# Normalizing rows before the transposes, with ScalarE forming the scaled high parts, in a hybrid S5/FNet encoder block on one Trainium2 core

## The chip, the cores and the metric

The kernel runs on one core of a Trainium2 chip. The metric is the device time of one execution in microseconds (us), the median of several runs. Engines are named as in the profile: PE is TensorE (PEld its weight loads), DVE is VectorE, ACT is ScalarE, POOL is GpSimd, SP is the queue that issues most loads. Rows that end in q (SPq, ACTq) are a queue's own instructions.

## The reference, cut to what matters

The model width is 2048, the sequence 512, the batch 1. All arrays are float32.

```python
mod = silu(c) @ w_ada + b_ada                       # six sections of 2048: sh_m, sc_m, g_m, sh_f, sc_f, g_f
h = rms_norm(x, norm_mix) * (1.0 + sc_m) + sh_m     # rms_norm: x * rsqrt(mean(x*x, -1) + 1e-6) * g
proj = h @ w_in                                     # widths: 512 (S5), 1536 (FNet), 2048 + 2048 (two gates)
merged = sigmoid(gate_s5) * (y_s5 @ w_branch_s5) + sigmoid(gate_fn) * (y_fn @ w_branch_fnet)
x = x + g_m * (merged @ w_out)                      # y_s5: bidirectional state-space scan; y_fn: 2-D DFT
h2 = rms_norm(x, norm_ffn) * (1.0 + sc_f) + sh_f
a, b = split(h2 @ w_ffn_in); x = x + g_f * ((silu(a) * b) @ w_ffn_out)
return rms_norm(x, norm_final)
```

## The kernel before, in words

Every large product is made of three fp32r matmuls (`mm3`, lines 207 to 209): each operand is split into a high part (`hi`, rounded to fp32r by ACT, line 124) and a low part (`lo`, source minus high part, by DVE, line 125). Activations are held transposed, as 16 pairs of tiles `h_hl[k]` of 128 channels x 512 positions (`actA` for k below 4, else `actB`).

Work is a list of steps. A step has a job (a load into a ring of buffers, then a preparation such as a split) and a function that issues the matmuls. `run_plan` walks the list and issues loads as soon as a ring slot is free: `raw` has 5 slots, `araw` 8, split weights (`whi`, `wlo`) 3. PE and POOL keep the order in which the program is written; the order on ACT, DVE and SP is set by the scheduler of the build.

The start, up to about 115 us, is this. `x_job(t)` loads a tile of 128 rows of x in two halves, transposes it on PE into `mg` (named `xT` in the rows), and squares it on ACT to get row sums. `x_rstd` turns all 512 sums into reciprocal roots and spreads them by matmuls into `rb` (128 x 512, the same in every partition). The scale section `sc_m` of `mod` is computed in five blocks of 256 to 512 columns, of which the first is done by PE (`ada_pe`) and the others by DVE, ACT and POOL (`ada_job`: DVE multiplies and adds, line 295; ACT scales and POOL adds a share of it, lines 289 and 291), and is summed over partitions by PE (line 340). Each finished block lets `form_hs(k)` make `h_hl[k]` from x times scale, still without the shift. Six column blocks of `w_in` (`start_w`) are multiplied as the k become ready. DVE does the scaled x (`scaled_x`, line 424, into `htmp`).

Then come column blocks 6 to 11 of the first gate (`ntile`). Beside them the shift section is computed (same `ada_job`), DVE works through small operations for the S5 tables (line 527), and during block 11 `form_h(k)` makes `h_hl[k]` anew, with the shift. After it `u_fn` computes the S5 input from eight weight tiles, here called u0 to u7. Between its matmuls PE transposes nine small tiles `dup` (line 670, written by ACT, lines 661 and 662, three buffers). SP loads the S5 arrays `R` (line 721) into memory that `mg` and the `dup` tiles used before. From `R`, DVE and POOL build the tables of eight S5 batches (lines 738 to 787), which PE takes up at lines 827, 863 and 901 to 904.

Much later, at 927 to 1127 us, block n of the product with `w_out` (lines 1342 to 1357) adds the old x, which comes back from DRAM (`sxT`) in tiles `xr`. Beside it DVE still computes scale and shift sections through the five `raw` slots.

Of the kernel before, what the change touches and what calls it, by code (L numbers as in the profile page):

```python
# [11 lines left out]
F32 = mybir.dt.float32  # L12
# [39 lines left out]
def encoder_block(ctx: ExitStack, tc: tile.TileContext, x, c, w_ada, b_ada, norm_mix, w_in,  # L52
# [174 lines left out]
    pv = ps_m((P, P))  # L227
    PE.transpose(pv, rows, ident)
    V.tensor_copy(vec, pv)
# [75 lines left out]
    def ada_pe(width, then):  # L305
# [5 lines left out]
        def job(q):  # L311
# [5 lines left out]
            def fn(r):  # L317
# [7 lines left out]
                if q == parts - 1:  # L325
                    n = width // P
                    V.tensor_reduce(out=mod[1][:, 0:n], in_=pt[0], op=ALU.add, axis=mybir.AxisListType.X)
                    V.tensor_tensor(out=mod[1][:, 0:n], in0=mod[1][:, 0:n], in1=vec[:, KT:KT + n], op=ALU.add)
                    then()
# [43 lines left out]
    rb = y_pool.tile([P, S], F32, name="rb")  # L373

    def x_job(t):
# [9 lines left out]
        def prep(r):  # L385
# [10 lines left out]
            for h in range(2):  # L396
                junk = ring.tile([P, D // 2], F32R, tag="whi", bufs=WH_BUFS, name="junk")
                A.activation(out=junk, in_=r[h], func=AF.Square, accum_out=xs_[:, h, t:t + 1])
            return None

        return Job(load, prep, raw=(("raw" if t < 2 else "araw", 2),), keep=())

    def x_rstd(_):
        v, r, t = (xs_[:, i, :] for i in (2, 3, 1))
        V.tensor_tensor(out=v, in0=xs_[:, 0, :], in1=xs_[:, 1, :], op=ALU.add)
        V.tensor_scalar(out=v, in0=v, scalar1=1.0 / D, scalar2=EPS, op0=ALU.mult, op1=ALU.add)
        newton_rsqrt(r, v, t)
        bcast_cols(r, rb)
# [6 lines left out]
    def form_hs(k):  # L415
# [3 lines left out]
        split(hi, lo, scaled_x(k))  # L419
        h_hl[k] = (hi, lo)  # L420

    def scaled_x(k):
        tmp = cpool.tile([P, S], F32, tag="tmp", bufs=3, name="htmp")
        V.scalar_tensor_tensor(out=tmp, in0=mg[:, k, :], scalar=s_mix[:, k:k + 1], in1=rb,
                               op0=ALU.mult, op1=ALU.mult)
        return tmp

    def form_h(k):
        add_split(h_hl[k], scaled_x(k), mod[0][:, k:k + 1])
# [30 lines left out]
    for i, (k0, nk) in enumerate(blocks):  # L460
# [4 lines left out]
        blk = ada_pe(nk * P, then) if i == 0 else ada_steps(1, k0 * P, nk * P, True, then)  # L465
# [4 lines left out]
        if i == 0:  # L470
            start_steps += [(x_job(t), nop) for t in range(4)]
            start_steps += blk[:-1] + [(None, x_rstd)] + blk[-1:] + ws
# [843 lines left out]
    def wo_open(_):  # L1316
# [8 lines left out]
        x1["x"] = {}  # L1325

    step(None, wo_open)

    def xT_load(n):
        xr = x1["p"].tile([P, S], F32, tag="xr", bufs=3, name="xr")  # L1330
        A.dma_start(out=xr, in_=sxT[n])
        x1["x"][n] = xr
# [444 lines left out]
```

## Time and profile before

| | |
|---|---|
| median of 3 runs (lowest, highest) | 2557.15 us (2549.0, 2558.74) |
| profiled execution: time, span | 2563.62 us, 2561.7 us |
| PE busy, share of the span | 2437.8 us, 95% |
| DVE busy | 1674.1 us, 65% |
| ACT busy | 1030.5 us, 40% |
| POOL busy | 605.9 us, 24% |
| PE, DVE busy at 30 to 130 us | 82.90, 90.96 us |
| PE, DVE busy at 130 to 200 us | 60.72, 65.53 us |

The span is that of one execution, 1.9 us shorter than its own time, and that time is 6.5 us above the median. PE is busy almost throughout, but a busy PE can run at the lower of its two clocks (1.2 instead of 2.4 GHz), which the windows show as a granted clock below 1.00. The first 200 us are where PE has gaps and DVE has almost none.

### The profile page before, as it was taken

Reading aid. Unit: us, or ns where it says so; the run is one execution under the profiler, and the core shown is the slowest. Engines: PE = TensorE matmul, PEld = TensorE weight load, DVE = VectorE, ACT = ScalarE, POOL = GpSimd, SP = SyncE. Lnnn points to the kernel's source line nnn. Section 1 sums busy time; section 2 is a strip of 40 time slices with the busy share of each in tenths; the row PEclk is TensorE's granted clock in tenths of the full one; section 3 lists DMA queues with packets and bytes.
Section 4 is the critical chain, followed back from the end, with each engine's and each line's share of the span. In section 5 each row is a group of like instructions: output and inputs, shape, how many; then the busy total and the mean of one; then the engine's idle time right before and its main releaser. Section 6 shows DMA issues by size and latency. Waiting matters only on the chain.

```text
span 2561.7 us, 37880 instructions
## 1 busy us (share of the span) xinstructions
PE 2437.8 (95%) x14475; PEld 2157.9 (84%) x14475; DVE 1674.1 (65%) x2454; ACT 1030.5 (40%) x1465; POOL 605.9 (24%) x683
## 2 busy tenths in 40 slices
PE   6989799899999899999999999999999999999997
PEld 5767687788888787778999999999999988888886
DVE  6998466537766987778567676776766643344335
ACT  4434333343223422244455555554555532223223
POOL 2441989600004510000222222222222230001001
PEclk8989999999999999999999999999999999999998
DMA  9796522558764678863888888888888984444442
GB/s 325 256 310 146 128 77 84 173 151 264 259 216 148 178 222 268 276 222 115 198 204 208 210 212 209 215 209 214 214 201 193 208 290 144 148 136 153 144 147 90
DMA packets 440901, 497.37 MB, mean 194 GB/s; under 512 B 51056, under 2 KB 336256, under 8 KB 440720
## 3 DMA queue, kind: packets, MB, share of 16 engines
q1 hardware_dynamic: 359472, 384.68, 47.6%
q0 software_dynamic: 52960, 79.78, 16.9%
q10 hardware_dynamic: 28288, 30.49, 4.1%
q8 instruction: 113, 1.85, 0.3%
q14 instruction: 68, 0.56, 0.1%
HBM read 395.17 MB, written 40.90 MB: 170 GB/s over the span
## 4 chain that ended last, share of the span: by engine, by line
PE 50%; DVE 18%; DMA 14%; issue 7%; POOL 6%; ACT 4%; SPq 0%; ACTq 0%; DVEq 0%; POOLq 0%
DMA raw<-in_w_ada_dram 6%; PE ps_acc L207 4%; PE ps_acc L208 4%; PE ps_acc L209 4%; DMA raw<-in_w_out_dram 3%; PE ps_acc L1656 3%; PE ps_acc L1655 3%; PE ps_acc L1657 3%; DVE ada L295 3%; DVE wlo L125 3%; PE ps_acc L1509 3%; PE ps_acc L1510 3%; PE ps_acc L1511 3%; DMA raw<-in_w_in_dram 2%; DVE lT L125 2%
## 5 line engine op out<-in xcount | busy, mean ns | idle before, releaser
L125 DVE TENSOR_TENSOR wlo<-raw,whi 128x1024 fp32r<-128x1024 f32 (+2 forms) x264 | 324.8, 1232 | 191.1 <-ACT whi L124 190.3
L1463 POOL DMA_DIRECT2D wlo<-raw x160 | 192.4, 1203 | 948.6 <-ACT wlo L1462 566.6
L124 ACT CAST whi<-raw 128x1024 fp32r<-128x1024 f32 (+2 forms) x264 | 260.5, 988 | 326.9 <-DMA raw<-in_w_out_dram 104.6
L209 PE MATMUL ps_acc<-actB,wlo 128*128 128x512 f32 x816 | 324.9, 398 | 8.1 <-DVE wlo L125 8.1
L207 PE MATMUL ps_acc<-actB,whi 128*128 128x512 f32 x816 | 329.9, 404 | 1.9 <-ACT whi L124 1.5
L208 PE MATMUL ps_acc<-actB,whi 128*128 128x512 f32 x816 | 324.1, 397 | 0.3 <-DVE actB L125 0.3
L124 ACT CAST hT<-raw 128x1024 fp32r<-128x1024 f32 x160 | 167.6, 1047 | 258.4 <-DVE raw L1474 174.0
L295 DVE SCALAR_TENSOR_TENSOR ada<-raw,c_s,ada 128x512 f32<-128x512 f32 x240 | 181.2, 755 | 134.2 <-DMA raw<-in_w_ada_dram 130.7
L125 DVE TENSOR_TENSOR lT<-raw,hT 128x1024 fp32r<-128x1024 f32 x160 | 195.5, 1222 | 79.2 <-ACT hT L124 78.9
L125 DVE TENSOR_TENSOR actA<-ab,actA 128x512 fp32r<-128x512 f32 x88 | 61.8, 704 | 263.2 <-ACT actA L124 263.2
L209 PEld LDWEIGHTS ps_acc<-actB,wlo 128*128 128x128 f32 x816 | 156.9, 192 | 45.3 <-DVE wlo L125 11.3
L207 PEld LDWEIGHTS ps_acc<-actB,whi 128*128 128x128 f32 x816 | 157.8, 193 | 37.0 <-ACT whi L124 2.7
L208 PEld LDWEIGHTS ps_acc<-actB,whi 128*128 128x128 f32 x816 | 157.1, 193 | 31.4 <-DVE actB L125 0.6
L124 ACT CAST actA<-ab 128x512 fp32r<-128x512 f32 x88 | 54.8, 623 | 315.3 <-PE ps_m L1656 305.6
L1461 ACT CAST whi<-raw 128x768 fp32r<-128x768 f32 x160 | 133.0, 831 | 90.7 <-PE ps_acc L1510 71.8
L1656 PE MATMUL ps_acc<-wlo,actA 128*128 128x512 f32 x352 | 137.2, 390 | 0.8 <-DVE wlo L125 0.8
L1655 PE MATMUL ps_acc<-whi,actA 128*128 128x512 f32 x352 | 137.2, 390 | 0.2 <-DVE ab L1521 0.2
L1657 PE MATMUL ps_acc<-whi,actA 128*128 128x512 f32 x352 | 137.0, 389 | 0.0
L1462 ACT ACTIVATE wlo<-raw 128x768 fp32r<-128x768 f32 x160 | 134.4, 840 | 0.0
L1675 POOL TENSOR_TENSOR actB<-actB 128x512 f32<-128x512 f32 x15 | 23.3, 1573 | 428.0 <-ACT fot L1673 428.0
L1472 DVE TENSOR_TENSOR raw<-raw 128x512 f32<-128x512 f32 x160 | 110.6, 691 | 18.9 <-DMA wlo<-raw 14.0
L207 PE MATMUL ps_acc<-actA,whi 128*128 128x512 f32 x272 | 112.9, 415 | 2.1 <-ACT actA L124 2.1
(475 smaller groups left out, 7049.2 us busy)
## 6 DMA issues: line engine op xcount, KB each, us to landing
raw<-in_w_ffn_in_dram SPq DMA_DIRECT2D x168, 512.0 KB
raw<-in_w_ada_dram SPq DMA_DIRECT2D x128, 512.0 KB
wlo<-raw POOLq DMA_DIRECT2D x160, 384.0 KB, 5.7
raw<-in_w_in_dram SPq DMA_DIRECT2D x108, 512.0 KB
raw<-in_w_ffn_out_dram SPq DMA_DIRECT2D x88, 512.0 KB
araw<-in_w_ada_dram SPq DMA_DIRECT2D x64, 512.0 KB
ab<-sg SPq DMA_DIRECT2D x88, 256.0 KB
raw<-in_w_out_dram SPq DMA_DIRECT2D x32, 512.0 KB
```

The lines of the kernel that those rows point to most:

```text
L124: A.copy(hi, src)
L125: V.tensor_tensor(out=lo, in0=src, in1=hi.bitcast(F32), op=ALU.subtract)
L207: PE.matmul(o, whi, ahi, start=start, stop=False)
L208: PE.matmul(o, whi, alo, start=False, stop=False)
L209: PE.matmul(o, wlo, ahi, start=False, stop=stop)
L295: V.scalar_tensor_tensor(out=acc, in0=r[:, k, :], scalar=sc, in1=acc, op0=ALU.mult, op1=ALU.add)
L1461: A.copy(hi, r[:, :, 0:3])
L1462: A.activation(out=lo, in_=r[:, :, 0:3], func=AF.Copy, scale=-1.0)
L1463: G.dma_start(out=lo, in_=r[:, :, 0:3], accum_op=ALU.add)
L1655: PE.matmul(o, gh[:, ts_], hi[:, cs], start=(k == 0), stop=False)
L1656: PE.matmul(o, gh[:, ts_], lo[:, cs], start=False, stop=False)
L1657: PE.matmul(o, gl[:, ts_], hi[:, cs], start=False, stop=(k == NF - 1))
```

## The change

Four things change. The first scale block (four `araw` loads) is loaded before x, and its matmuls come first on PE. Each tile of x is normalized as it lies: the reciprocal root is formed for each tile by itself, DVE multiplies the first half of the rows and ACT the second, and the transposes follow, so `mg` holds normalized x, and `rb` is gone. In `form_hs` ACT writes the high part directly from `mg` with the scale, and DVE the low part, with no `htmp`; in `form_h` ACT writes `htmp` (scale and shift), and again the high part. At the product with `w_out` the stored x must be multiplied back by its root mean square: `sd` is spread by matmuls at its beginning, and POOL multiplies each `xr` tile by it. A scheduler barrier stands behind the x tiles.

```diff
-    pv = ps_m((P, P))
-    PE.transpose(pv, rows, ident)
-    V.tensor_copy(vec, pv)
+    def vec_t():
+        pv = ps_m((P, P))
+        PE.transpose(pv, rows, ident)
+        V.tensor_copy(vec, pv)
...
                 if q == parts - 1:
+                    vec_t()
...
-        def prep(r):
+        def fn(r):
+            s0, s1, v, rstd = (xs_[:, i, t:t + 1] for i in range(4))
+            for h in range(2):
+                junk = ring.tile([P, D // 2], F32R, tag="whi", bufs=WH_BUFS, name="junk")
+                A.activation(out=junk, in_=r[h], func=AF.Square, accum_out=xs_[:, h, t:t + 1])
+            V.tensor_tensor(out=v, in0=s0, in1=s1, op=ALU.add)
+            V.tensor_scalar(out=v, in0=v, scalar1=1.0 / D, scalar2=EPS, op0=ALU.mult, op1=ALU.add)
+            newton_rsqrt(rstd, v, s1)
+            V.tensor_scalar(out=r[0], in0=r[0], scalar1=rstd, scalar2=None, op0=ALU.mult)
+            A.activation(out=r[1], in_=r[1], func=AF.Copy, scale=rstd)
             for q in range(4):
...
+            V.tensor_tensor(out=s0, in0=v, in1=rstd, op=ALU.mult)
+        return Job(load, lambda r: r, raw=(("raw" if t < 2 else "araw", 2),), keep=(), hold=True), fn
...
-        split(hi, lo, scaled_x(k))
+        sc = s_mix[:, k:k + 1]
+        A.activation(out=hi, in_=mg[:, k, :], func=AF.Copy, scale=sc)
+        V.scalar_tensor_tensor(out=lo, in0=mg[:, k, :], scalar=sc, in1=hi.bitcast(F32),
+                               op0=ALU.mult, op1=ALU.subtract)
...
-    def scaled_x(k):
+    def form_h(k):
         tmp = cpool.tile([P, S], F32, tag="tmp", bufs=3, name="htmp")
-        V.scalar_tensor_tensor(out=tmp, in0=mg[:, k, :], scalar=s_mix[:, k:k + 1], in1=rb,
-                               op0=ALU.mult, op1=ALU.mult)
-        return tmp
-    def form_h(k):
-        add_split(h_hl[k], scaled_x(k), mod[0][:, k:k + 1])
+        A.activation(out=tmp, in_=mg[:, k, :], func=AF.Identity, scale=s_mix[:, k:k + 1],
+                     bias=mod[0][:, k:k + 1])
+        split(*h_hl[k], tmp)
...
-            start_steps += [(x_job(t), nop) for t in range(4)]
-            start_steps += blk[:-1] + [(None, x_rstd)] + blk[-1:] + ws
+            start_steps += blk + [x_job(t) for t in range(4)]
+            barriers.add(len(start_steps))
+            start_steps += [(None, lambda _, then=then: (tc.no_sync_barrier(), then()))] + ws
...
+        x1["sd"] = p.tile([P, S], F32, name="sd")
+        bcast_cols(xs_[:, 0, :], x1["sd"])
...
         A.dma_start(out=xr, in_=sxT[n])
+        G.tensor_tensor(out=xr, in0=xr, in1=x1["sd"], op=ALU.mult)
```

On ACT at the start of the program, before the change, the squares and copies of the x tiles (`junk`, `xT`) stand in this order up to the first weight split and the first high part of h (`actA`):

```order
L398 ACTIVATE junk,xs<-raw 128x1024 x4
L398 ACTIVATE junk,xs<-xr 128x1024
L393 COPY xT<-ps_acc 128x4x128
L398 ACTIVATE junk,xs<-xr 128x1024 x2
L393 COPY xT<-ps_acc 128x4x128
L398 ACTIVATE junk,xs<-xr 128x1024
L393 COPY xT<-ps_acc 128x4x128 x2
L235 ACT_TABLE_LOAD
L235 ACTIVATE xs<-xs 128x4
```

With the change, the second half of the same stretch on ACT, from the last squares to the first high part, reads (L397 multiplies half a tile of x, L237 is a square root):

```order
L397 ACTIVATE raw<-raw,xs 128x1024
L392 ACTIVATE junk,xs<-xr 128x1024 x2
L405 COPY xT<-ps_acc 128x4x128
L397 ACTIVATE xr<-xr,xs 128x1024
L237 ACTIVATE xs<-xs 128x1
L405 COPY xT<-ps_acc 128x4x128
L397 ACTIVATE xr<-xr,xs 128x1024
L405 COPY xT<-ps_acc 128x4x128
L124 CAST whi<-raw 128x768
L423 ACTIVATE actA<-xT,s_mix 128x512
```

Four multiplications and four square roots now stand between the squares, and the copies wait for transposes that wait for a multiplication.

On ACT during block 11, before the change, the high parts of `form_h` (L128), the weight splits and the `dup` tiles are mixed:

```order
L128 ACTIVATE actB<-htmp,mod_91 128x512 x3
L124 CAST whi<-raw 128x1024
L128 ACTIVATE actB<-htmp,mod_91 128x512 x3
L661 ACTIVATE dup<-q_1124 64x64
L128 ACTIVATE actB<-htmp,mod_91 128x512
L662 ACTIVATE dup<-q_1124 64x64
L124 CAST whi<-raw 128x1024
L661 ACTIVATE dup<-q_1123 64x64
```

With the change the same place on ACT has `htmp` and high parts of all 16 k in a row, with one weight split between them; these are its last rows and what follows:

```order
L430 ACTIVATE htmp<-xT,mod_88,s_mix 128x512 x2
L124 CAST actB<-htmp 128x512 x2
L455 COPY sg<-ps_acc 128x512
L124 CAST whi<-raw 128x1024
L458 DMA sg_100<-sg 128x512
L665 ACTIVATE dup<-q_1122 64x64
L666 ACTIVATE dup<-q_1122 64x64
L124 CAST whi<-raw 128x1024
L665 ACTIVATE dup<-q_1121 64x64
```

The fourth `dup` tile moved from behind the tenth high part to behind the sixteenth, the copy of block 11 and a weight split. On SP, before the change, the loads of `R` stand so between the loads of u0 to u7 (128x2x512) and of the blocks after them:

```order
L137 DMA raw<-in_w_in_dram 128x2x512 x7
L721 DMA R<-in_s_b_re_dram 64x32x16
L137 DMA raw<-in_w_in_dram 128x2x512
L721 DMA R<-in_s_b_im_dram 64x32x16
L137 DMA raw<-in_w_in_dram 128x8x128 x2
L721 DMA R<-in_s_b_im_dram 64x32x16
```

and with the change so:

```order
L137 DMA raw<-in_w_in_dram 128x2x512 x8
L137 DMA raw<-in_w_in_dram 128x8x128
L725 DMA R<-in_s_b_re_dram 64x32x16
L725 DMA R<-in_s_b_im_dram 64x32x16 x2
L137 DMA raw<-in_w_in_dram 128x8x128
L725 DMA R<-in_s_b_re_dram 64x32x16 x2
```

The first `R` load moved behind two more weight loads. Behind the second load of 128x8x128 stood six `R` loads before, and five stand there now. Behind these places the order on all engines is the same as before, but for the spreading matmuls and the POOL multiplications at the product with `w_out`.

## Rows read from the trace of the kernel before

**Rows 1.** The page, part 1: busy time, share of the span, instructions.

```profile
PE 2437.8 (95%) x14475; PEld 2157.9 (84%) x14475; DVE 1674.1 (65%) x2454; ACT 1030.5 (40%) x1465; POOL 605.9 (24%) x683
```

**Rows 2.** Windows: stretch, length, busy time of each engine (instructions), PEclk, DMA share, GB/s.

```profile
10.00:20.00 10.00, 10.00 (x81) 9.79 (x79) 7.78 (x14) 8.08 (x15) 0.00 (x0) 1.00 1.06 376
...
30.00:130.00 100.00, 82.90 (x333) 66.97 (x334) 90.96 (x118) 44.65 (x70) 42.38 (x31) 0.87 0.81 273
130.00:200.00 70.00, 60.72 (x249) 47.71 (x248) 65.53 (x172) 24.81 (x39) 29.80 (x19) 0.90 0.91 305
```

**Rows 3.** Groups by shape on DVE at 28 to 135 us: busy, mean ns | idle.

```profile
L424 DVE SCALAR_TENSOR_TENSOR htmp<-xT,s_mix,rb 128x512 f32<-128x512 f32 x16 | 13.0, 840 | 0.0
```

**Rows 4.** The chain that ended last, within the first 330 us: start, us, what.

```profile
126.41 6.93 DMA ls<-in_s_log_step_dram
```

**Rows 5.** Timeline of the first 62 us: start, us, engine, line, operation [idle before].

```profile
5.42 1.04 ACT L398 ACTIVATE junk<-raw 128x1024 fp32r<-128x1024 f32 x1
...
14.13 3.84 PE L390 MATMUL ps_acc<-ident,xr 128*128 128x128 f32 x32
...
20.22 0.20 ACT L235 ACTIVATE xs<-xs 128x4 f32<-128x4 f32 x1
...
21.27 0.16 DVE L240 TENSOR_TENSOR xs<-xs 128x4 f32<-128x4 f32 x1
...
21.36 0.96 DVE L125 TENSOR_TENSOR wlo<-raw,whi 128x768 fp32r<-128x768 f32 x1
...
23.37 2.05 PE L246 MATMUL ps_m<-ident,xs 128*128 128x128 f32 x8
...
30.74 0.79 PE L207 MATMUL ps_acc<-actA,whi 128*128 128x512 f32 x1 [2.11 <-ACT actA L124]
```

**Rows 6.** Groups by shape on ACT at 5 to 31 us: count | busy, mean ns | idle.

```profile
L235 ACT ACT_TABLE_LOAD x1 | 1.3, 1283 | 0.3 <-DVE xs L406 0.3
```

**Rows 7.** Timeline of ACT, DVE and PE at 196 to 262 us.

```profile
201.12 0.58 ACT L452 COPY sg<-ps_acc 128x512 f32<-128x512 f32 x1
...
216.84 1.39 ACT L128 ACTIVATE actB<-htmp,mod 128x512 fp32r<-128x512 f32 x2 [2.16 <-DVE htmp L424]
...
206.30 0.75 DVE L424 SCALAR_TENSOR_TENSOR htmp<-xT,s_mix,rb 128x512 f32<-128x512 f32 x1 [1.85 <-DMA sg<-sg]
...
219.44 0.27 PE L670 MATMUL ps_m<-ident,dup 64*128 64x64 f32 x1
```

**Rows 8.** The chain at 200 to 640 us, around the S5 tables.

```profile
233.28 0.68 SPq L721
...
242.07 4.85 DMA R<-in_s_b_re_dram
...
316.60 0.69 PE ps_accb L902 x2
```

**Rows 9.** Waits of PE at 230 to 620 us: waited for, us in total, times, longest.

```profile
PE ps_accb L902 <- POOL S L887: 11.9, 2, 11.4
```

**Rows 10.** Windows of PE alone: stretch, length, busy (instructions), PEclk, DMA share, GB/s.

```profile
320.00:330.00 10.00, 10.00 (x39) 0.67 0.00 0
330.00:340.00 10.00, 10.00 (x56) 1.00 0.25 79
```

**Rows 11.** The chain at 1006 to 1032 us, in the product with w_out.

```profile
1014.84 1.06 ACT whi L124
1015.92 1.24 DVE wlo L125
1017.18 3.90 DMA raw<-in_w_out_dram
...
1030.24 0.67 DVE x1T L1345
```

**Rows 12.** Instructions on the araw tiles to 130 us: ns min/median/max, first and last start.

```profile
L295 DVE SCALAR_TENSOR_TENSOR ada<-araw,c_s,ada x42: 478/752/1789, 31.0 to 125.5; 128x512 f32<-128x512 f32 x35, 128x256 f32<-128x256 f32 x7
L291 POOL TENSOR_TENSOR ada<-ada,araw x27: 777/1614/2153, 32.0 to 123.2; 128x512 f32<-128x512 f32 x20, 128x256 f32<-128x256 f32 x7
```

More of the change, by code (lines that the diff above doesn't have):

```diff
@@ L372, in encoder_block @@
     xs_ = cpool.tile([P, 4, 4], F32, name="xs")
-    rb = y_pool.tile([P, S], F32, name="rb")
     def x_job(t):
@@ L395, in prep @@
                     V.tensor_copy(dst, pt)
[L396 to L408, printed above, removed]
+            V.tensor_tensor(out=s0, in0=v, in1=rstd, op=ALU.mult)
+        return Job(load, lambda r: r, raw=(("raw" if t < 2 else "araw", 2),), keep=(), hold=True), fn
     h_hl = [None] * KT
@@ L463, in then @@
                 form_hs(k)
-        blk = ada_pe(nk * P, then) if i == 0 else ada_steps(1, k0 * P, nk * P, True, then)
+        blk = ada_pe(nk * P, lambda: None) if i == 0 else ada_steps(1, k0 * P, nk * P, True, then)
         ws = []
```

## The prediction

> **What bounds the kernel now.** The page comes first: PE is busy for 95% of the span [rows 1], so a change pays only where PE waits or what PE waits for comes sooner. The windows show where that is: at 30 to 130 us PE is busy for 82.90 of 100 us at a granted clock of 0.87, and DVE for 90.96; at 130 to 200 us the two have 60.72 and 65.53 of 70 [rows 2]. In these 170 us DVE is the fullest engine. It is not the only limit: the chain leaves it for DMA and POOL in places, such as the 6.93 us for a small S5 array at 126 us [rows 4].
>
> Next comes a stretch in which PE does not set the end, though it looks busy. The chain at 200 to 640 us runs from the load of R, which lands about 247 us (242.07 + 4.85), through POOL to PE at 316.60 us [rows 8]. PE itself had waited 11.4 us there for POOL [rows 9]. So between about 201 us (the end of block 10, [rows 7]) and 316 us there are two lines: PE's, with 11.4 us to spare, and that of R, with nothing to spare. The third view is the chain in the product with w_out: there it never passes PE, but goes round load, ACT split, DVE split, load [rows 11]. There a slower DVE costs time too.
>
> **The change part by part**, as gains (-) and losses (+) in us.
>
> *The first matmul of start_w, at 30.74 us now* [rows 5]. Before, ACT had the squares done early, and PE's own list (transposes, scale block, spreading) set the time. Now ACT is the line. Half tiles of x are squared from 5.42 us on [rows 5]; four loads of 512 KB stand ahead now, at 376 GB/s [rows 2] 1.4 us each, so the first is squared at about 11.0 us. Until its first high part ACT does eight squares of 1.04 [rows 5], four multiplications of the same shape (taken at 1.04), four copies like the 0.58 of another [rows 7], one table load of 1.28 [rows 6], four roots of 0.20 [rows 5], a weight split (at most the 1.06 of a larger one, [rows 11]) and the high part (0.7, from [rows 7]): 18.6 us. Without a wait the matmuls begin at 11.0 + 18.6 = 29.6 us, 1.1 earlier than now. There will be waits: sum, root, DVE's small operations, multiplication, transposes and copy now follow each other within a tile, and DVE's list has the same chain in order. For the last tile I add one such chain that ACT cannot cover: some 1.2 for the DVE operations after the root (20.22 to 21.43 us now) and 1.9 for 16 transposes (half of 3.84), with some 0.6 for DVE's order [rows 5]: 33.3 us, or **+2.6** (bounds -1.1 and +4).
>
> *Scaled x.* Sixteen operations of 13.0 us in all go from DVE [rows 3]; the low part becomes an operation of the kind and size of the one that goes, and 1.0 us is left for what it costs more than the subtraction that it replaces. One weight split of 0.96 us that lay in DVE's idle time at 21.36 us [rows 5] falls behind the barrier. That leaves 11 us of DVE. If DVE set the time throughout, all 11 would come back; where loads or POOL set it, none. I take 65%, **-7.2** (bounds 0 and -11), since DVE is 92% busy over the 170 us but the chain goes elsewhere in part. Block 11 then begins 4.6 us earlier.
>
> *form_h in block 11.* DVE loses 16 operations here too, but ACT gets 16 more. Let T be the end of block 10, 201.1 us. From there ACT copies block 10 (0.6), makes 16 htmp and 16 high parts at a pitch of 0.67 (1.39 less 0.72 for two, [rows 7]), 21.4 us, waits about 2.5 us for the copy's store before the third htmp, since htmp shares its three buffers (DVE waits there now until 206.30, [rows 7]), makes two weight splits of 1.06, the copy of block 11 and the fourth dup, 0.5: about T + 27.7. PE wants the fourth dup at 219.44 [rows 7], T + 18.3, between matmuls of u1. It will wait there some **9 us** (bounds 6 and 11). This wait falls on the line that has 11.4 us to spare, so its own price is 0 as long as R is not late. What is queued behind it: dup tiles 5 to 9 on PE, the end of u1, and so the split of u4 and the weight load ahead of the last five R loads.
>
> *R.* Now it lands at T + 46. With the change the first R loads go when u3 is split and the last dup is read (about T + 31), the other five when u4 is split (after u1, T + 34, plus 1.06 and 1.2 for its splits): about T + 36.5. Six took from 233.28 to 247 us [rows 8], with a weight load or two in front; five should take some 10.5: T + 47, **+1** (bounds -3 and +5). The rest of the S5 part follows R.
>
> *PE's clock at 316 us.* After its 11.4 us of waiting PE runs at the lower clock: 39 instructions in ten us at 0.67, 56 in the next ten at 1.00 [rows 10]. With PE arriving only some 2 us early that goes, and the chain passes PE there: 17 instructions of 0.23 us, less one for a short dip, **-3** (bounds 0 and -4). The same dip after the new wait lies in the spare time.
>
> *POOL's multiplications of xr.* Sixteen, of the shape of line 291. Alone they cost nothing: an xr tile is fetched a block ahead. But where DVE and POOL work at once, DVE's ada operation takes up to 1.79 us against 0.75, beside POOL's 1.61 [rows 12]: 1.03 more. Over one round of the w_out chain, from x1T at some 1006.9 to x1T at 1030.24 us, DVE holds it for three splits of 1.24, one x1T of 0.67 and two ada of 0.75 [rows 12], 5.9 of 23.4 us or 25% [rows 11]. 16 x 0.25 x 1.03 = **+4** (bounds 0 and 16.5, if every one meets the chain). The Trainium skill, page "SBUF — State Buffer", section "Who interferes with whom", says that a DVE instruction with two SBUF inputs and a GpSimd instruction that reads SBUF lock each other out for a whole instruction. The 1.03 us above agrees with it. By that rule alone every multiplication that meets a DVE operation is paid in full, the +16.5 of the upper bound and the time of rival B.
>
> *The spreading.* Eight PE instructions of 2.05 us at the start [rows 5] are inside the first term; at the w_out product, at the full clock, about half: **+1** (0 to 2).
>
> *At nothing:* the four smaller edits (vec_t, the DVE multiplications before 33 us, the sd column, the memory of rb) lie in DVE's or PE's idle time of the first 30 us, where DVE works 7.78 of ten us at most [rows 2].
>
> Sum: 2.6 - 7.2 + 1 - 3 + 4 + 1 = -1.6. The profiled execution took 2563.6 us and would become 2562.0; the median of the runs shown is 6.5 us lower, so 2555.5, said as **2556 us**.
>
> **The rivals.**
>
> *A, the start pays in full:* DVE sets the time throughout (-11), ACT does not wait (0 against +2.6), POOL meets nothing in the chain. -11 + 1 - 3 + 1 = -12: 2545. For it: DVE's 90.96 of 100; against it: POOL and DMA on the chain.
>
> *B, slower, by POOL at the w_out product:* the multiplications meet the chain each time. +16.5 for +4: 2568. It decides from 0.35 us for each multiplication on (all other terms give -5.6). For it: the rows of the start, where DVE and POOL take turns; against it: DVE idles there while the loads come.
>
> *C, the wait for dup is not swallowed:* R comes T + 51 instead of T + 47, and PE idles at 316 us again (+4 + 3): 2563.
>
> *D, the relief does not act:* loads set the pace (376 GB/s is all they reach, [rows 2]), so only the losses stay: +7.2: 2563.
>
> **How the numbers follow.** The forecast gets 0.45, A 0.16, B 0.16, C 0.13, D 0.10. Its own range is 2549 to 2562. The range from 2542 to 2569 takes in A and most of B and leaves out about 2 in 10 of the spread around them. About 0.5% (12.8 us) is what a measurement of this kernel can tell from no change; below 2544.4 lie half of A and a tail (0.13), above 2569.9 less than half of B and a tail (0.09); the rest is 0.78.
>
> **What would show it.** The first L207 at 32 to 34 us; PE's gap up to the end of block 10 shorter, that end near 196.5 us; a PE wait of 6 to 11 us for a dup tile, and the wait for S in 902's line down to 3 us or less; the product with w_out 1 to 10 us longer than its 200 us, with DVE operations of 1.7 us beside POOL. Wrong would be: no PE wait for dup; the S wait still 11 us; a w_out product of more than 210 us; an end of block 10 not earlier than 201 us.

## The result, and the profile after

The changed kernel takes 2580.14 us (median of 6 runs, 2576.84 to 2594.64) and the kernel before 2560.42 beside it: the ratio is 1.0085 with a 95% interval from 1.0061 to 1.0110. That is 20 us slower, where 2556 was forecast with a range from 2542 to 2569. The profiled execution took 2583.76 us, with a span of 2582.0.

The page's part 1 for the changed kernel, beside [rows 1]:

```profile
PE 2450.8 (95%) x14475; PEld 2169.4 (84%) x14475; DVE 1674.5 (65%) x2451; ACT 1044.6 (40%) x1488; POOL 622.2 (24%) x699
```

The shares are those of before; totals don't show a change that moves waits. The windows of the changed kernel, in the columns of [rows 2]:

```profile
10.00:20.00 10.00, 9.79 (x46) 9.50 (x46) 0.36 (x2) 2.30 (x4) 0.00 (x0) 1.00 1.02 411
30.00:130.00 100.00, 74.18 (x326) 60.54 (x324) 83.22 (x124) 47.41 (x75) 37.94 (x31) 0.89 0.75 261
130.00:200.00 70.00, 60.29 (x262) 48.97 (x263) 61.72 (x157) 27.89 (x45) 26.52 (x19) 0.91 0.92 312
```

At 10 to 20 us DVE works 0.36 us where it worked 7.78, and ACT 2.30 for 8.08. At 30 to 130 us DVE is less busy, as wanted, but PE is too, by 8.7 us, and the loads move 261 GB/s for 273. The start has become late. The timelines of PE, DVE and ACT show why (start, us, engine, line, operation, idle time before and what ended it):

```profile
5.69 13.79 PE L325 MATMUL ps_accb<-c_s,araw 128*128 128x1 f32 x64 [5.69 <-DMA araw<-in_w_ada_dram]
12.88 1.06 ACT L392 ACTIVATE junk<-raw 128x1024 fp32r<-128x1024 f32 x1
19.52 0.19 DVE L330 TENSOR_REDUCE mod<-ps_accb 128x2 f32<-128x32 f32 x1 [18.26 <-PE ps_accb L325]
20.24 0.15 DVE L393 TENSOR_TENSOR xs<-xs 128x1 f32<-128x1 f32 x1
20.66 1.28 ACT L237 ACT_TABLE_LOAD   x1 [6.63 <-DVE xs L394]
23.97 3.68 PE L402 MATMUL ps_acc<-ident,raw 128*128 128x128 f32 x16 [4.17 <-DVE raw L396]
38.74 1.94 PE L402 MATMUL ps_acc<-ident,xr 128*128 128x128 f32 x16 [1.69 <-DVE xr L396]
41.35 0.48 DVE L295 TENSOR_SCALAR ada<-araw,c_s 128x512 f32<-128x512 f32 x1
42.71 0.50 PE L207 MATMUL ps_acc<-actA,whi 128*128 128x512 f32 x1 [2.03 <-ACT actA L423]
```

Tile 0 has its squares by 14.0 us, but its sum (L393) stands in DVE's list behind the fold of the scale block (L330), which waits until PE is through with that block. So sum, root, multiplication and transposes all start about 6 us late. Of the 12.6 us that ACT waits from its first square on, 6.63 are this one wait. Then the chain inside a tile comes four times: PE's transposes go from 23.97 to 40.7 us. The first matmul of start_w comes at 42.71 us, not at 30.74 [rows 5] or the forecast's 33.3.

The end of block 10 and block 11, from the timelines of ACT and PE, beside [rows 7]:

```profile
210.97 0.58 ACT L455 COPY sg<-ps_acc 128x512 f32<-128x512 f32 x1
211.44 0.82 ACT L430 ACTIVATE htmp<-xT,mod,s_mix 128x512 f32<-128x512 f32 x1
...
230.32 1.52 ACT L430 ACTIVATE htmp<-xT,mod,s_mix 128x512 f32<-128x512 f32 x2
...
232.77 0.58 ACT L455 COPY sg<-ps_acc 128x512 f32<-128x512 f32 x1
...
234.19 0.27 ACT L665 ACTIVATE dup<-q 64x64 f32<-64x64 f32 x1
...
234.66 0.37 PE L674 MATMUL ps_m<-ident,dup 64*128 64x64 f32 x1 [5.30 <-ACT dup L666]
234.95 0.80 PE L207 MATMUL ps_acc<-actA,whi 128*128 128x512 f32 x1
```

ACT's list of htmp and high parts runs to 232.8 us, and only then comes the dup for which PE has waited 5.30 us. Behind the wait PE runs at a lower clock; windows of PE alone (length, busy, PEclk, DMA share, GB/s):

```profile
220.00:230.00 10.00, 9.36 (x39) 1.00 0.15 52
230.00:240.00 10.00, 5.34 (x12) 0.57 0.38 116
240.00:250.00 10.00, 10.00 (x26) 0.57 0.45 55
...
235.00:240.00 5.00, 5.00 (x12) 0.50 0.61 179
244.00:248.00 4.00, 4.00 (x11) 0.50 0.49 48
```

The 0.57 of the windows of 10 us is a mean. From 235 to 248 us the granted clock is 0.50, the lower level of 1.2 GHz, and a matmul starts every 0.43 us; after 248.3 us one starts every 0.23 us again. PE lies 9.85 us behind the execution of before at 228.73 us and 21.15 behind at 250.04: the dup costs 11.3 us, half of it wait and half clock. The loads of R follow; the chain, beside [rows 8], and the waits of PE at 230 to 640 us, beside [rows 9]:

```profile
250.33 4.01 SPq L725
...
257.22 4.85 DMA R<-in_s_b_re_dram
```
```profile
PE ps_accb L906 <- POOL E L771: 4.9, 3, 2.1
PE ps_accb L906 <- DVE S L894: 2.3, 2, 1.1
```

R lands at 262.07 us, 51.1 us behind the end of block 10 instead of 46. PE's wait of 11.4 us for S is gone, since PE itself is late now, and the end doesn't come sooner for it: POOL's first table operation starts at 263.18 us for 247.98, 15.2 later, and its operations at 340 to 500 us stay 13 to 19 us, most of them 14 to 16 us, behind those of before.

### The profile page after: what moved, and what is told of

Same layout as the page of the kernel before. It is cut to its first block, busy times and chain, and to the rows that moved or that the text cites. A ratio compares the mean times of both kernels' runs of the same rounds, so it can differ in the third digit from the quotient of the medians.

```text
span 2582.0 us, 37958 instructions
## 1 busy us (share of the span) xinstructions
PE 2450.8 (95%) x14475; PEld 2169.4 (84%) x14475; DVE 1674.5 (65%) x2451; ACT 1044.6 (40%) x1488; POOL 622.2 (24%) x699
## 3 DMA queue, kind: packets, MB, share of 16 engines
q1 hardware_dynamic: 359472, 384.68, 46.9%
## 4 chain that ended last, share of the span: by engine, by line
PE 52%; DVE 17%; DMA 15%; issue 8%; ACT 4%; POOL 3%; SPq 1%; ACTq 0%; DVEq 0%; POOLq 0%
DMA raw<-in_w_ada_dram 5%; PE ps_acc L207 4%; PE ps_acc L209 4%; PE ps_acc L208 4%; DVE ada L297 4%; PE ps_acc L1663 3%; PE ps_acc L1517 3%; PE ps_acc L1664 3%; PE ps_acc L1516 3%; PE ps_acc L1662 3%; PE ps_acc L1518 3%; DVE wlo L125 3%; DMA raw<-in_w_out_dram 3%; DMA raw<-in_w_in_dram 3%; DMA wlo<-raw 2%
## 5 line engine op out<-in xcount | busy, mean ns | idle before, releaser
L125 DVE TENSOR_TENSOR wlo<-raw,whi 128x1024 fp32r<-128x1024 f32 (+2 forms) x264 | 333.1, 1263 | 199.1 <-ACT whi L124 192.2
L207 PE MATMUL ps_acc<-actB,whi 128*128 128x512 f32 x816 | 327.9, 402 | 3.2 <-ACT actB L423 3.2
L297 DVE SCALAR_TENSOR_TENSOR ada<-raw,c_s,ada 128x512 f32<-128x512 f32 x240 | 187.1, 780 | 134.4 <-DMA raw<-in_w_ada_dram 130.9
L207 PEld LDWEIGHTS ps_acc<-actB,whi 128*128 128x128 f32 x816 | 156.4, 192 | 37.2 <-ACT actB L423 4.0
L207 PE MATMUL ps_acc<-actA,whi 128*128 128x512 f32 x272 | 116.4, 428 | 2.0 <-ACT actA L423 2.0
```

What stands on the lines that cost most here:

```text
L125: V.tensor_tensor(out=lo, in0=src, in1=hi.bitcast(F32), op=ALU.subtract)
L207: PE.matmul(o, whi, ahi, start=start, stop=False)
L297: V.scalar_tensor_tensor(out=acc, in0=r[:, k, :], scalar=sc, in1=acc, op0=ALU.mult, op1=ALU.add)
```

## The experiments

All ratios are to the kernel before, run on the same chip. One profile is one execution: the three profiles of programs that are the changed kernel up to the product with w_out put the end of block 10 at 207.4, 209.7 and 211.0 us. From the last x1T on, where all kernels here do the same work, the profiles take 1428 to 1444 us. So stages are compared by their profiles, and totals by the ratios. Read from the timelines, in us: the first L207, DVE's first scale operation of the second block (L295, L293 in the kernel before; "first ada"), the copy of block 10 (its end), the difference of these two, and how far behind the end the last load of R is issued.

| kernel | L207 | first ada | end of 10 | difference | last R | ratio (95%) |
|---|---|---|---|---|---|---|
| before | 30.7 | 30.0 | 201.1 | 171.2 | 41.0 | 1 |
| changed | 42.7 | 41.4 | 211.0 | 169.6 | 46.3 | 1.0085 (61 to 110) |
| after_again | 42.1 | 40.3 | 209.7 | 169.4 | 44.1 | 1.0073 (51 to 94) |
| no_back | 41.7 | 40.4 | 207.4 | 167.1 | 47.0 | 1.0056 (36 to 76) |
| fold_late | 40.1 | 35.9 | 202.7 | 166.8 | 44.3 | 1.0046 (27 to 64) |
| x_inter | 35.8 | 35.0 | 203.9 | 168.9 | 43.1 | 1.0045 (26 to 64) |
| x_own | 38.2 | 37.4 | 205.7 | 168.3 | 45.9 | 1.0028 (2 to 54) |
| dve_hs | 42.0 | 40.1 | 208.6 | 168.4 | 46.7 | 1.0063 (43 to 83) |
| more_dve | 41.1 | 39.3 | 208.1 | 168.8 | 44.7 | 1.0070 (47 to 94) |
| more_load | 42.4 | 40.3 | 214.6 | 174.3 | 47.1 | 1.0082 (55 to 109) |
| no_alo | 41.5 | 39.4 | 202.9 | 163.5 | 46.4 | 1.0039 (16 to 62) |
| araw6 | 42.0 | 40.6 | 203.3 | 162.7 | 45.9 | 1.0058 (35 to 81) |
| pooled2 | 41.9 | 39.8 | 196.7 | 156.9 | 46.9 | 1.0025 (2 to 49) |
| dve_h | 41.2 | 39.1 | 208.4 | 169.3 | 37.3 | 1.0026 (5 to 48) |
| xi_h | 38.5 | 37.6 | 206.3 | 168.7 | 37.4 | 1.0018 (0 to 37) |
| x_own_h | 38.9 | 38.1 | 206.5 | 168.4 | 37.2 | 0.9998 (-27 to 23) |
| batch_h | 40.4 | 39.6 | 211.2 | 171.5 | 38.2 | 1.0039 (21 to 58) |
| before_p2 | 30.5 | 29.7 | 196.8 | 167.1 | 41.0 | 0.9969 (-51 to -11) |
| xi_h_p2 | 36.3 | 35.4 | 194.2 | 158.8 | 38.5 | 0.9985 (-34 to 5) |
| xi_h_p1 | 36.4 | 35.5 | 183.2 | 147.7 | 37.6 | 0.9950 (-66 to -34) |

(Intervals in ten thousandths from 1.)

**after_again**, the changed kernel again. 

> The changed kernel once more, unaltered, beside the others on one chip. If its extra time is that of the kernel and not of one execution, its ratio to before lies at 1.006 to 1.011 again, the first matmul of start_w at 41 to 43 us and the end of block 10 at 208 to 212 us. If it was the execution, the ratio falls to 1.004 to 1.006, where two of the variants stood, and these two times move with it.

 It is the kernel, not one execution: 1.0073.

### The start

**fold_late**

```diff
                 if q == parts - 1:
+                    folds.append(fold)
+            def fold():
                     vec_t()
...
-            start_steps += [(None, lambda _, then=then: (tc.no_sync_barrier(), then()))] + ws
+            start_steps += [(None, lambda _, then=then: (tc.no_sync_barrier(), folds.pop()(), then()))] + ws
```

> The changed kernel, with the fold of the first scale block (its sum over PE's columns, the transpose of the rows and the sum with vec) put behind the four tiles of x. Theory one: DVE, which works its list in order, held tile 0 of x back because that fold stood ahead of it and waited 18.3 us for PE's scale block; with the fold behind, tile 0's sum starts at about 14.1 us instead of 20.2 (its squares end at 14.0), and the first matmul of start_w comes at about 36.6 us instead of 42.7. Theory two: the loads ahead of x alone cost the start, and the later tiles set its end; then the first matmul stays at 41 to 43 us. What reaches the end is 2 to 6 us of the 6 by theory one (about 2575), 0 by theory two (2580).

Tile 0's sum did start as theory one has it, at 14.37 us. But the first matmul gained 1.6 to 2.6 us against the three profiles of the changed start, not 6. DVE and PE in its timelines:

```profile
14.37 0.16 DVE L398 TENSOR_TENSOR xs<-xs 128x1 f32<-128x1 f32 x1 [13.11 <-ACT junk L397]
19.53 3.65 PE L407 MATMUL ps_acc<-ident,raw 128*128 128x128 f32 x16
35.88 0.48 DVE L295 TENSOR_SCALAR ada<-araw,c_s 128x512 f32<-128x512 f32 x1
40.10 0.79 PE L207 MATMUL ps_acc<-actA,whi 128*128 128x512 f32 x1 [4.74 <-ACT actA L428]
```

PE's scale block holds the transposes until 19.53 us, so a second wait stands right behind the first. And the fold, now behind the tiles, is late itself: DVE makes the scale column (`s_mix`) only at 38.08 us, and PE waits 4.74 us for the high part made with it. DVE's first scale operation gained 4.4 to 5.5 us, and the end of block 10 4.7 to 8.3.

**x_inter**, and **x_own** on top of it:

```diff
-  start_steps += blk + [x_job(t) for t in range(4)]
+  start_steps += [s for t in range(4) for s in (x_job(t), blk[t])]
   # x_own also:
-  r = [raw_tile(...) / y_pool.tile(..., tag="araw") for _ in range(2)]
+  r = [act_tile(4, F32) for _ in range(4)]   # loads, squares and multiplications in quarters of a tile
```

> The changed kernel, with the order of the start undone: a tile of x, then a quarter of the first scale block, four times over, in loads and in work; the normalization by rows stays. If order (loads ahead of x 6.2 us, DVE's wait behind the scale block 6.1 us) is what put the first matmul of start_w at 42.7 us, it comes at 30 to 32 us now, and the kernel takes 2568 to 2574 us. If the chain within a tile (sum, root, four small operations, multiplication, transposes, copies) is what costs the time, it comes at 36 us or later and the kernel stays within 5 us of 2580.

> The variant with x and scale block interleaved, and now x is loaded into 16 tiles of the pool of the activations' high and low parts (idle then) instead of the buffers that the scale and weight loads use. Theory one: between the first matmul of start_w and the end of block 10 the loads set the pace, and tiles of x that sit in their buffers until they are normalized keep them back (the five scale loads behind x were issued by 35.8 us in the changed kernel, 28.0 with the interleaving, 20.0 before). Then they are issued by 18 us, the end of block 10 comes at 193 to 200 us instead of 203.4 with the interleaving alone, and the whole time is 4 to 9 us lower than that variant's ratio of 1.0045 (so 0.999 to 1.003). Theory two: the chain within each tile of x sets it; then the end of block 10 stays at 202 us or later and the ratio at 1.0045.

x_inter's first matmul came at 35.81 us, between the two; three later kernels with the same start have it at 36.3, 36.4 and 38.5. Order is worth 3 to 7 us of the 11 to 12, and 5 to 8 are left. PE in x_inter:

```profile
11.94 3.65 PE L402 MATMUL ps_acc<-ident,raw 128*128 128x128 f32 x16 [11.94 <-DVE xs L409]
...
28.27 2.40 PE L402 MATMUL ps_acc<-ident,xr 128*128 128x128 f32 x16 [0.63 <-DVE xr L396]
30.46 3.41 PE L325 MATMUL ps_accb<-c_s,araw 128*128 128x1 f32 x16
```

It starts transposing at 11.94 us, where the kernel before starts at 8.81, since tile 0 must be normalized first; it waits for DVE at two later tiles (1.38 and 0.63 us), and ends its scale block at 33.9 us for 28.6. That accounts for the 5 us of this profile. The scheduler barrier behind the tiles stayed in every variant and was not tested. With x_own the five scale loads behind x were issued by 21.1 us instead of 28.0, later than the 18 that its theory one counted on, but block 10 ended no earlier (205.7). So theory one found no support: an earlier issue of these loads did not bring block 10 forward.

**batch_h**: one root for the four tiles, with form_h as in dve_h below.

```diff
+  start_steps += [x_job(t) for t in range(4)] + blk[:-1] + [(None, x_rest)] + blk[-1:]
   # x_job: squares only; x_rest: sum and newton_rsqrt on 128x4, then scale, transpose and copy (ACT two of four)
```

> The changed kernel with three things altered: x loads ahead of the scale block again, the roots of all four tiles of x are taken together (squares of all tiles, one table load, one root, then scaling, transposes and copies tile by tile, two copies of four on ACT), and form_h is as before (DVE forms the scaled tile). If the chain of sum, root and small operations repeated in each tile is what still held the first matmul of start_w at 35.8 us with the order undone, it comes at 29 to 33 us now, the end of block 10 at 195 to 199 us, R lands 42 to 44 us behind it, and the ratio to before is 0.994 to 0.999. If the start was not held by that chain, the first matmul stays at 35 us or later and the ratio at 1.000 (as with x in tiles of its own).

A miss, and PE's timeline says why:

```profile
16.67 10.37 PE L325 MATMUL ps_accb<-c_s,araw 128*128 128x1 f32 x48 [16.67 <-DMA araw<-in_w_ada_dram]
26.90 6.54 PE L413 MATMUL ps_acc<-ident,raw 128*128 128x128 f32 x32
33.28 3.79 PE L413 MATMUL ps_acc<-ident,xr 128*128 128x128 f32 x32
```

The roots are there at 19.2 us, but PE works on the scale block until 27. Before, it transposed raw rows from 8.81 us on. With the normalization of all tiles ahead of the transposes PE has nothing to do until the scale block's loads land at 16.67 us, and then both jobs stand behind each other. The repeated chain was not tested apart from this.

### From the first scale operation to the end of block 10

The difference in the table is 171.2 us before and 166.8 to 171.5 in all variants that move the start or form_h: a late start is passed on nearly whole. What sets it?

**dve_hs**, **more_dve**, **more_load**:

```diff
   # dve_hs, form_hs
-  A.activation(out=hi, in_=mg[:, k, :], func=AF.Copy, scale=sc); V.scalar_tensor_tensor(out=lo, ...)
+  V.tensor_scalar(out=tmp, in0=mg[:, k, :], scalar1=sc, scalar2=None, op0=ALU.mult); split(hi, lo, tmp)
   # more_dve, form_hs
+  V.scalar_tensor_tensor(out=more, in0=mg[:, k, :], scalar=sc, in1=mg[:, k, :], ...)
   # more_load, start_w, k from 3 to 12
+  nc.sync.dma_start(out=smore[k - 3], in_=w_ada_v[:, 0:2, (k - 3) * S:(k - 2) * S])
```

> The changed kernel, but in start_w's preparation DVE again forms the scaled tile (16 operations of some 0.5 us, one input) and ACT copies it for the high part. This undoes the relief of DVE alone. Theory one: DVE sets the pace between the first matmul (42.7 us) and the end of block 10 (211.0 us); then that stretch of 168.3 us becomes 4 to 8 us longer. Theory two: loads and other waits set the pace there; then it stays within 2 us of 168.3, and so does the whole time of 2580.

> The changed kernel with 16 more DVE operations in start_w's preparation, one behind each low part, of its kind and size (0.75 us, 12 us in all; their output is not used). Three profiles of the changed kernel's start put 163.1 to 167.9 us less or more between the first matmul of start_w and the end of block 10 (before: 169.8). Theory one: DVE sets the pace there; the stretch grows by 8 to 12 us, to 172 us or more. Theory two: DVE has slack there, which is why giving it 16 operations less brought nothing; the stretch stays at 162 to 169 us and the time within 4 us of the changed kernel's.

> The changed kernel with ten more transfers of 512 KB each, of columns of w_ada to a scratch tensor in DRAM that nothing reads, issued one for each of start_w's k from 3 to 12. Theory one: loads set the pace between the first matmul of start_w and the end of block 10 (at 1.4 us for each 512 KB the ten take 14 us); the stretch grows by 8 us or more, from 163 to 168 us to 174 us or more. Theory two: something else sets it (PE's own work at the low clock, the order of the list on ACT and DVE); it grows by 3 us at most.

With the relief undone the difference is 168.4. In more_dve DVE is busy for 160.5 us of the stretch instead of 144.9, and the difference is 168.8. Both lie within the 167.1 to 169.6 of the three profiles: DVE had room, and the relief by itself is worth nothing that shows here. Ten more loads add 5 to 7 us of their 14, between the two theories.

**no_alo**, **araw6**, **pooled2**:

```diff
   # no_alo, in start_w only
-  mm3(acc0[n], (hi[:, cs], lo[:, cs]), h_hl[k], k == 0, k == KT - 1)
+  PE.matmul(acc0[n], hi[:, cs], h_hl[k][0], start=k == 0, stop=False)
+  PE.matmul(acc0[n], lo[:, cs], h_hl[k][0], start=False, stop=k == KT - 1)
-  ARAW_BUFS = 8
+  ARAW_BUFS = 6                        # araw6
-  POOLED = (1, 3, 5)
+  POOLED = (1, 3)                      # pooled2
```

> The changed kernel without the middle one of start_w's three products (high part of the weight by low part of the activation; 96 PE matmuls of 0.23 to 0.39 us, 22 us or more; the product is left out of the sum). From DVE's first scale operation of the second block to the end of block 10 the changed kernel takes 167.1 to 169.6 us (three profiles). Theory PE: its own work sets this length; it falls by 12 us or more. Theory loads: the turn of load, scale operation, free buffer, next load sets it; it falls by 4 us at most.

> The changed kernel with six buffers for the scale loads instead of eight. Theory loads by buffers: how many loads can be under way or wait sets the length of 167.1 to 169.6 us; it grows by 5 us or more. Theory loads by rate, or PE: it stays within 3 us. The start may come later too, since the tiles of x use the same buffers; the length is measured from DVE's first scale operation of the second block, so that is not in it.

> The changed kernel with two of eight loads of a scale block scaled by ACT and added by POOL instead of three; DVE takes the third (two operations of 0.75 us more for each block on DVE, two operations fewer on ACT and on POOL). Theory ACT and POOL: their part of a scale block sets the length of 167.1 to 169.6 us; it falls by 3 us or more. Theory loads: within 2 us of that. Theory DVE, already unlikely: it grows by 4 us or more.

no_alo gives 163.5, between its theories. araw6 gives 162.7, against both: fewer buffers made it shorter, which stays unexplained. pooled2 gives 156.9: of all that was tried, taking work from ACT and POOL shortens the stretch most. The stretch as one window, in the columns of [rows 2], changed kernel and then pooled2:

```profile
41.35:210.97 169.62, 136.11 (x589) 110.22 (x590) 144.93 (x279) 71.78 (x112) 65.57 (x50) 0.90 0.85 290
```
```profile
39.80:196.69 156.89, 134.96 (x590) 110.26 (x590) 143.29 (x293) 63.97 (x99) 45.52 (x36) 0.92 0.92 315
```

DVE does 14 operations more in 1.6 us less of busy time, and the loads run at 315 GB/s instead of 290, so 290 was not the most that they can do. Whether POOL's own line, the load buffers that it holds or the DVE operations beside it make the stretch long was not separated. DVE's groups by shape, changed kernel first, then pooled2, then xi_h_p1 (below):

```profile
L297 DVE SCALAR_TENSOR_TENSOR ada<-araw,c_s,ada 128x512 f32<-128x512 f32 x63 | 59.9, 956 | 1.9 <-DMA araw<-in_w_ada_dram 1.8
```
```profile
L297 DVE SCALAR_TENSOR_TENSOR ada<-araw,c_s,ada 128x512 f32<-128x512 f32 x77 | 63.5, 834 | 0.3
```
```profile
L297 DVE SCALAR_TENSOR_TENSOR ada<-araw,c_s,ada 128x512 f32<-128x512 f32 x91 | 69.3, 774 | 0.2
```

Fourteen operations taken from POOL cost DVE 3.6 us, the next fourteen 5.8: each of DVE's operations gets faster as POOL's grow fewer. The Trainium skill, page "SBUF — State Buffer", section "Who interferes with whom", gives DVE and GpSimd one shared pair of ports under an exclusive lock; the mean falling from 956 to 774 ns agrees with it.

**before_p2**, **xi_h_p2**, **xi_h_p1**: POOLED = (1, 3) in the kernel before; the same in xi_h (below); POOLED = (3,) in xi_h.

> The kernel before, with two of eight loads of a scale block on ACT and POOL instead of three. In the changed kernel this took 12 us from the stretch of 169 us. Theory one: DVE, 92% busy in this stretch before, has no room for it, and the relief is what made the room; the stretch of 171.2 us becomes at most 5 us shorter, or longer, and the ratio is 0.998 to 1.003. Theory two: DVE has room in either kernel; the stretch falls to 158 to 162 us here too and the ratio is 0.994 to 0.998.

> The changed kernel with tiles of x and quarters of the scale block interleaved, form_h as before, and two of eight loads of a scale block on ACT and POOL. If the three effects add up, the stretch is 155 to 159 us, the end of block 10 comes at 192 to 197 us, R lands 37 to 38 us (issue of its last load) behind it, and the ratio to before is 0.995 to 0.999: 12 us below the 1.0018 of the same kernel with three of eight, less what is swallowed later. If POOL's line in the S5 part or the product with w_out swallows it, the ratio stays above 1.000.

> The same with one of eight loads of a scale block on ACT and POOL. If ACT and POOL still set the length with two of eight, the stretch falls again, to 145 to 152 us, and the ratio lies some 0.002 to 0.004 below that of two of eight. If DVE or the loads take over there, the stretch stays at 155 us or longer and the ratio is no lower.

In the kernel before the difference falls by 4.1 us only, in the changed one by 10 to 13: in this stretch theory one holds, and the relief makes room once work is moved onto DVE. The total doesn't show it: before_p2 has 0.9969, below theory one's range, and xi_h_p2, in whose start and block 11 the losses are reduced, has 0.9985; the intervals overlap. With one of eight the difference falls to 147.7, as forecast, and the ratio to 0.9950 (0.9934 to 0.9966), a median of 2555.48 us beside 2567.63. That is faster than the kernel before, but its interval meets those of before_p2 and xi_h_p2. Its profiled execution, with a span of 2566.6, was the slowest of its 13. The kernel before with one of eight was not tried, so no gain of the change itself is shown.

### Block 11 and R

**dve_h**, and **xi_h**, **x_own_h** (x_inter and x_own with the same edit):

```diff
-  A.activation(out=tmp, in_=mg[:, k, :], func=AF.Identity, scale=s_mix[:, k:k + 1], bias=mod[0][:, k:k + 1])
-  split(*h_hl[k], tmp)
+  V.tensor_scalar(out=tmp, in0=mg[:, k, :], scalar1=s_mix[:, k:k + 1], scalar2=None, op0=ALU.mult)
+  add_split(h_hl[k], tmp, mod[0][:, k:k + 1])
```

> The changed kernel, but in block 11 form_h is as it was: DVE forms the scaled tile, ACT adds the column for the high part, DVE makes the low part. Theory one: ACT's second operation for each of 16 tiles makes the fourth dup late (PE waited 5.3 us and ran on at the low clock, 11.3 us lost in u1 in all), and with it the loads of R, which landed 51 us after block 10's end instead of 46. Then PE's wait for dup goes, R lands 46 to 47 us after block 10's end, PE waits for S again, and the time falls by 2 to 5 us to some 2576. Theory two, the one the forecast used: the wait lies in PE's spare time and R hardly depends on it; then the time stays at 2580.

> The changed kernel with the two largest causes undone together: tiles of x and quarters of the scale block interleaved, and form_h as before (DVE forms the scaled tile); normalization by rows, ACT's high parts and POOL's multiplications stay. If the two add up, the first matmul of start_w comes at 35 to 37 us, the end of block 10 at 202 to 205 us, R lands 42 to 44 us behind it, and the ratio to before is 0.998 to 1.002 (the start's rest of 2 to 3 us and POOL's 3 against 3 to 4 us from the faster form_h). If they overlap, so that undoing one had already given back most of the other, the ratio stays above 1.003.

> The variant with x in tiles of its own, and form_h as it was before (DVE forms the scaled tile). If the late start and the late fourth dup are the two causes that matter, with POOL's multiplications as a third of some 3 to 4 us, the end of block 10 comes at 193 to 200 us, R lands 42 to 47 us behind it, and the ratio to before is 0.996 to 1.000. If something else in the change costs the time, the ratio stays above 1.002.

PE's wait for dup is gone in dve_h, and in the six kernels with this edit the last load of R is issued 37.2 to 38.6 us behind block 10's end, against 43.1 to 47.1 with the changed form_h and 41.0 before. Instructions on htmp in dve_h, then in the changed kernel:

```profile
L430 DVE TENSOR_SCALAR htmp<-xT,s_mix x16: 477/481/487, 208.5 to 230.1; 128x512 f32<-128x512 f32 x16
L128 ACT ACTIVATE actB<-htmp,mod x12: 707/710/737, 215.4 to 233.1; 128x512 fp32r<-128x512 f32 x12
```
```profile
L430 ACT ACTIVATE htmp<-xT,mod,s_mix x16: 802/816/822, 211.4 to 231.0; 128x512 f32<-128x512 f32 x16
L124 ACT CAST actB<-htmp x12: 608/616/626, 217.8 to 232.2; 128x512 fp32r<-128x512 f32 x12
```

ACT has 0.71 us for a tile there instead of 0.82 + 0.62, and can put the dups between. Theory one of dve_h was right on the cause and too small in size: its last load of R is issued 37.3 us behind block 10, so R lands some 42 us behind it and not 46 to 47, and the ratio falls from 1.0073 and 1.0085 to 1.0026, 12 to 15 us where 2 to 5 were expected. But dve_h is not quite form_h as it was: without `rb` DVE's htmp has one input and takes 0.48 us, where it took 0.75 [rows 7], and R comes 3.7 us earlier behind block 10 than in the kernel before. So not all that dve_h gives back was lost by the change. xi_h and x_own_h take both causes away: 1.0018 and 0.9998, with block 10 ending later than either expectation had it (206.3 and 206.5).

### The product with w_out

**no_back**: `G.tensor_tensor(out=xr, in0=xr, in1=x1["sd"], op=ALU.mult)` left out.

> The changed kernel without POOL's multiplication of xr by sd ahead of the residual of the product with w_out (so the residual there is the normalized x, not x). Theory one: POOL's 16 multiplications slow DVE in the chain of that product; then the product, 3.7 us longer than before in the changed kernel, gets these back within 1 us, and the whole time falls by about 4 us against the changed kernel beside it. Theory two: the 3.7 us come from low clock stretches or loads of that execution; then the product keeps 2 us or more of them.

DVE's scale operations in that product, groups by shape, changed kernel and then no_back:

```profile
L297 DVE SCALAR_TENSOR_TENSOR ada<-raw,c_s,ada 128x512 f32<-128x512 f32 x108 | 87.5, 810 | 2.5
```
```profile
L297 DVE SCALAR_TENSOR_TENSOR ada<-raw,c_s,ada 128x512 f32<-128x512 f32 x108 | 80.9, 750 | 2.5
```

POOL's 16 multiplications cost DVE 6.6 us in these alone. The x1T of the product (first and last start), before, changed and no_back:

```profile
L1345 DVE SCALAR_TENSOR_TENSOR x1T<-ps_acc,mod,xr x16: 744/745/751, 939.8 to 1126.7; 128x512 f32<-128x512 f32 x16
```
```profile
L1352 DVE SCALAR_TENSOR_TENSOR x1T<-ps_acc,mod,xr x16: 743/746/751, 959.5 to 1149.0; 128x512 f32<-128x512 f32 x16
```
```profile
L1351 DVE SCALAR_TENSOR_TENSOR x1T<-ps_acc,mod,xr x16: 744/746/751, 955.8 to 1143.8; 128x512 f32<-128x512 f32 x16
```

From the first x1T to the last the product takes 186.9 us before, 189.5 in the changed kernel, 188.0 in no_back, and 186.7 to 193.4 in the 17 profiles with multiplication, 189.4 on average. By these means the multiplications cost the product 1.4 to 2.5 us, but single profiles with them are as short as 186.7, and the ratios of no_back and after_again (1.0056 and 1.0073, beside each other) overlap. Neither theory is settled.

## Why the prediction was wrong

Of the prediction's own signs of being wrong one came: block 10 ended at 207.4 to 211.0 us, not earlier than 201. Three steps failed, the start, the relief of DVE and R. By term of the sum:

- *The first matmul of start_w, +2.6*: the step that failed most. It came 12 us later. The squares began at 11.60 us as reckoned (11.0), but the sum let ACT's 18.6 us run with 3.7 us of waits, and the waits were 12.6. It had placed tile 0's chain in DVE's list without what stands ahead of it: the fold, waiting for PE. fold_late shows that this wait held tile 0 by 6 us, and x_inter that the order costs 3 to 7 us of the first matmul. The rest goes with the normalization that now stands ahead of PE's transposes; this is read from PE's timelines, and no variant takes the normalization away.
- *Scaled x, -7.2*: the end of block 10 was to gain from DVE's relief. The difference shrank by 1.6 to 4.1 us, and as much with the relief undone (dve_hs): rival D had this outcome, but not its reason. Loads at their full rate don't set the pace: they run at 290 GB/s in the stretch, at 315 in pooled2 and 330 in xi_h_p1, and ten more of them cost 5 to 7 of 14 us. (Nor were 376 GB/s all that they reach: at 20 to 30 us of the kernel before it is 384.) The step that failed was to take a share of 92% busy for the limit. More DVE work did not lengthen the stretch, and less POOL work shortened it.
- *form_h, priced 0*: the wait came (5.3 us; 6 to 11 forecast), and its low clock doubled it, which the sum left out. That it lies in PE's spare time was right for PE, which lost its wait for S, and wrong for R, whose loads stand behind u1: *R, +1* was +5 in this profile and +3 to +6 by the last issue of the three. Rival C gave T + 51, and R landed at T + 51.1. C and D were held to exclude each other; what came was R as late as in C and no gain as in D, with the late start on top.
- *PE's clock, -3*: the dip at S went, but the end gained nothing by it, since R and with it POOL's tables came 15 us later.
- *POOL's multiplications, +4*: DVE's operations did get slower beside POOL (810 ns for 750), but what that costs the end, 1.4 to 2.5 us by the means, is not clear of the spread of single profiles. The +1 for spreading was not measured by itself.

The spans of the two profiles differ by 20.3 us. Up to POOL's first table operation it is 15.2: 11.4 at the first scale operation, -1.6 in the stretch, 5.4 for R. From there to the first x1T it is 4.5 more (696.3 us for 691.8), in the product 2.6 more, and behind it 2.0 less. In the part of 691.8 us the variants of the changed kernel take 691 to 703 us, 4 us more than before on average. What that is stays open; it is about the spread of single executions.

## What to carry to other kernels

When a small operation is moved, look at what stands ahead of it in its engine's list and what that waits for: a fold of 0.2 us held DVE for 18, and the chain behind it for 6. The fullest engine need not be the limit: part of its time can be operations that are long because another engine works beside it. Give it more work in an experiment, and take work from its neighbour, before relieving it. A wait on a line with time to spare still counts for every load that is queued behind it.

## Not expected of the hardware

DVE's 128x512 scale operation takes 956 ns on average beside three eighths of the block's work on POOL, 834 beside two and 774 beside one; moving a 1.57 us addition from POOL to DVE cost DVE 0.26 to 0.41 us, though the operation that does it on DVE takes 0.75 us with POOL idle (no_back). After a PE wait of 5.3 us PE was busy without a gap from 235 us on, and still the granted clock was 0.50, the level of 1.2 GHz, until 248 us, with a matmul every 0.43 us instead of 0.23; the lower clock cost as much as the wait. And the same start gave the first matmul at 35.8 us in one kernel (x_inter) and 38.5 in another (xi_h).
